# Two token groups, 128 and 160 wide, at the ends and openings of the stages of a decoder trunk

## The chip, the core and the metric

The kernel runs on one core of one Trainium2 chip. A core has a matrix engine (TensorE, "PE" in the rows, with its weight loads listed apart as "PEld"), a vector engine (VectorE, "DVE"), an activation engine (ScalarE, "ACT"), GpSimd ("POOL") and queues for transfers (SP, and the queues of ACT and POOL). The metric is the device time of one execution in microseconds (us); less is better.

## The reference

One step of a two-layer decoder trunk over 288 token columns: 256 tokens of a prompt and 32 tokens of a sample group (8 sequences of 4). Everything is float32.

```python
for l in range(DEPTH):                       # DEPTH = 2
    h = rms_norm(x, norm_mix_pre[l])
    m = pool_sgu_mixer(h, ...) if l % 2 == 0 else retention_mixer(h, ...)
    x = x + rms_norm(m, norm_mix_post[l])
    h = rms_norm(x, norm_ffn_pre[l])
    f = conv_ffn(h, ...)                     # gelu(conv(h @ w_gate)) * (h @ w_up) @ w_down
    x = x + rms_norm(f, norm_ffn_post[l])

def rms_norm(x, g):
    return x * lax.rsqrt(jnp.mean(x * x, axis=-1, keepdims=True) + EPS) * g
```

What matters here: between two stages stands a norm over all 2048 features of a token, so the first product of a stage needs the last product of the stage before, for the same token. Different tokens don't need each other in a norm.

## The kernel before

Features lie on the partitions (16 tiles of 128) and the 288 tokens on the free axis. `xbuf` (tiles `x[k]`) holds the residual, `mbuf` (`m`) the output of a stage before its norm, `hh[k]` and `hl[k]` the rounded part and the rest of the normed input of a stage. Every product is made in blocks of 128 x 128 weights. `mm3` (L198) makes three matmuls of a block: rounded weights by rounded input (L201), rounded weights by the rest of the input (L203, or L205 where it is put off to the end of a first pass), rest of the weights by rounded input (L206). All three move 288 columns, each with a weight load of its own of 128 columns. There are 6928 blocks; their weights come in chunks of 8 blocks (512 KB) in one fixed order, written out by `block` (L152): ACT rounds a chunk (`whi`, L134) and DVE takes the rest (`wlo`, L141), up to four chunks ahead (`wsp`, 4 buffers).

`product` (L212) makes the output tiles of one product. The first `first` tiles (`acc_h`) run side by side, input tile by input tile, so that the matmuls of input tile kk follow as soon as `prep(kk)` has made that tile; the other tiles (`acc_n`) run one after the other. Work of the other engines is written into this stream by hand: `tick()` after each block steps generators that yield for a number of blocks.

Three times a stage ends in a norm and another one opens on it: the mixer of layer 0 into its feed-forward part, that into the retention mixer of layer 1, that into the second feed-forward part. A fourth end is that of the kernel. At each of them the last product (`add_out`, L381) squares its tiles and adds the squares up on POOL (`sqm`); `post_stat` (L359) sums the squares over the partitions by narrow matmuls (`rms_stat`, `st_ps`, L289 and L292), DVE and POOL make the inverse root (`ms` L295, `rs` L297), and `rms_bcast` spreads it over the partitions by matmuls (`rb_ps`, L306). In the meantime TensorE runs matmuls on zeros (`keep_warm`, L274; at the end of the retention mixer `final_state` of the last head, L820 to L822, stands in the place of two of the three groups). Then `entry` (L330) makes the input of the next stage tile by tile: DVE scales `m` by the norm (`pn`, L377), DVE or POOL adds it to `x` (L378), ACT makes `hh` (L342) and squares (L314), DVE makes `hl` (L345). The first five tiles of the next product (`HEAD = 5`) follow this through 16 passes, one for each input tile. The second norm (before a stage) is not waited for: it is made beside the last passes (`rb_side`) and multiplied into the outputs. At the end of the kernel the same scaling and adding (L987, L991) leads to the stores of `y` (L992).

Of the kernel before, what the change touches and what calls it, by code (L numbers as in the profile page):

```python
# [14 lines left out]
D = 2048  # L15
# [15 lines left out]
HEAD = 5  # L31
TAIL = ((0, 1, 1), (1, 1, 0), (2, 2, 1), (4, 1, 0), (5, 2, 1), (7, 1, 0), (8, 1, 0), (9, 2, 1), (11, 1, 0), (12, 1, 1), (13, 2, 0), (15, 1, 0))
# [74 lines left out]
def trunk(ctx: ExitStack, tc: tile.TileContext, i, o, g4, order):  # L107
# [13 lines left out]
    state = {"loaded": 0, "hi": 0, "lo": 0, "next": 0}  # L121
# [22 lines left out]
    def prefetch(loads, his, los):  # L144
        while state["loaded"] < min(loads, NCHUNK):
            load_chunk()
        while state["hi"] < min(his, NCHUNK):
            hi_chunk()
        while state["lo"] < min(los, NCHUNK):
            lo_chunk()  # L150

    def block(mat, kt, nt):  # L152
# [7 lines left out]
        if b == 1:  # L160
            prefetch(c + 7, c + 4, 0)
        if b == 5:
            prefetch(0, 0, c + 4)
        hi, lo = chunks[c]
        return hi[:, b * 128:(b + 1) * 128], lo[:, b * 128:(b + 1) * 128]
# [42 lines left out]

    def bank(name):
        return psum.tile([128, 512], F32, tag="ps", name=name)  # L210

    def product(nts, kts, rhs, evac, first=0, prep=None, begin=None):  # L212
# [3 lines left out]
        for kk, kt in enumerate(kts):  # L216
# [10 lines left out]
        for j in range(len(head), len(nts)):  # L227
# [7 lines left out]
        drain("evac")  # L235
# [49 lines left out]
    def rms_stat(parts):  # L285

        ps = bank("st_ps")
        zeros = wz.bitcast(F32)
        PE.matmul(ps[0:96, 0:6], zeros[:, 0:96], zeros[:, 0:6], start=True, stop=False)  # L289
        for n, sq in enumerate(parts):  # L290
            for t in range(3):
                PE.matmul(ps[0:96, 2 * t:2 * t + 2], sq[:, 96 * t:96 * t + 96], ones[:, 0:2],  # L292
                          start=False, stop=n == len(parts) - 1 and t == 2)
        ms = tmp.tile([96, 3], F32, tag="ms", name="ms")
        V.tensor_scalar(ms, ps[0:96, 0:6].rearrange("p (t c) -> p t c", c=2)[:, :, 0], 1.0 / D, EPS, op0=ALU.mult, op1=ALU.add)  # L295
        rs = tmp.tile([96, 3], F32, tag="rs", name="rs")
        G.tensor_tensor(rs, ms, mhalf[0:96, 0:3], op=ALU.pow)  # L297
        return rs

    def rms_bcast(rs):  # L300

        pb = bank("rb_ps")
        for t in range(3):
            r = rs[:, t:t + 1]
            r = bass.AP(tensor=r.tensor, offset=r.offset, ap=[list(r.ap[0]), [0, 128]])
            PE.matmul(pb[:, 96 * t:96 * t + 96], r, ident[0:96, 0:96], start=True, stop=True)  # L306
        return pb[:, 0:T]
# [22 lines left out]
    def entry(gain, update, ahead):  # L330

        sq = t288("sq2", tag="sq")
        box = []
        done = [0]

        def upto(n):
            while done[0] < min(n, KT + 2):
                k = done[0]
                if k < KT:
                    update(k)  # L340
                if 1 <= k <= KT:
                    A.activation(hh[k - 1], x[k - 1], AF.Copy, scale=col(gain, k - 1))  # L342
                    square_add(sq, x[k - 1], k - 1)
                if k >= 2:
                    V.scalar_tensor_tensor(hl[k - 2], x[k - 2], col(gain, k - 2), hh[k - 2].bitcast(F32),  # L345
                                           op0=ALU.mult, op1=ALU.subtract)
                done[0] += 1
                if done[0] == KT + 2:
                    side("fast", late(rb_side(sq, box)))
# [5 lines left out]
        def prep(kk):  # L355
            upto(kk + 3 + ahead)
        return prep, box

    def post_stat(parts, fill=None):  # L359
        drain("late")  # L360
        if fill:
            fill[0]()
        else:
            keep_warm(6)
        rs = rms_stat(parts)
        if fill:
            fill[1]()
        else:
            keep_warm(5)
        pb = rms_bcast(rs)  # L370
        keep_warm(7)
        return pb

    def post_update(pb):
        def update(k):
# [3 lines left out]
        return update  # L379

    def add_out(first, parts=None, gain=None):  # L381

        def evac(j, ps):
# [11 lines left out]
        def squared(j, ps):  # L395
            if j < KT - 1:
                yield 1
# [3 lines left out]
            elif j < KT - 1:  # L401
                square_add(parts[0], ps, j)
            else:
                s = t288("sqt", tag="t2")
                A.activation(s, ps, AF.Square)
                parts.append(s)
# [11 lines left out]
    with ExitStack() as l0:  # L418
        p0 = l0.enter_context(tc.tile_pool(name="p0", bufs=1))
        hid = l0.enter_context(tc.tile_pool(name="hid0", bufs=16))  # L420
        prep, rbox = entry("pre_mix0", lambda k: prefetch(3, (k + 1) // 3, k // 3), 2)
# [45 lines left out]
        def v_norm():  # L467
# [18 lines left out]
            for t, n in ((0, 128), (1, 128), (2, 32)):  # L486
                vt = vtok[0:n, t, :]
                V.tensor_tensor(vt, vt, sgb[0:n, :], op=ALU.add)
                yield 14
            G.dma_start(out=o["cv"], in_=vtok[0:32, 2, :])  # L490
# [43 lines left out]
        def mix(j):  # L534
            yield 3
            h = j // 2
            pm = bank("mix_ps")
# [26 lines left out]
        def begin_mix(j):  # L564
            if j >= 16:
# [3 lines left out]
                first=HEAD, prep=prep, begin=begin_mix)  # L569
# [10 lines left out]
        for gi in range(4):  # L580
# [3 lines left out]
        parts = []  # L584
# [6 lines left out]
    def ffn(l, pb):  # L591
        with ExitStack() as s:
            pf = s.enter_context(tc.tile_pool(name=f"pf{l}", bufs=1))
            hid = s.enter_context(tc.tile_pool(name=f"hidf{l}", bufs=GRP + 3))
            prep, rbox = entry(f"pre_ffn{l}", post_update(pb), 2)
# [5 lines left out]
            G.dma_start(out=cs, in_=i["conv"][l])  # L601
            for ex in exts:
                G.memset(ex[:, 0:2], 0.0)
            hsp, gl = {}, {}

# [37 lines left out]
            def pairs(fs, first=0, prep=None):  # L643
                product([(f"{w}{l}", f) for f in fs for w in ("gate", "up")], ALLK, hs,
                        lambda j, ps: (evac_gate, evac_up)[j % 2](fs[j // 2], ps), first=first, prep=prep)

            NG = FT // GRP
            parts = []
            for g in range(NG):
# [5 lines left out]
                if g + 1 < NG:  # L655
                    pairs([fs[-1] + 1])
                drain("late")
                product([(f"down{l}", n) for n in ALLK], fs, hsp, add_out(g == 0, parts if g == NG - 1 else None, f"post_ffn{l}"),
                        first=4 if g == NG - 1 else 0)
            G.dma_start(out=o["conv"][l], in_=co)  # L660
            return post_stat(parts)

    pb = ffn(0, pb)


    with ExitStack() as l1:
        hid = l1.enter_context(tc.tile_pool(name="hid1", bufs=8))
        p1 = l1.enter_context(tc.tile_pool(name="p1", bufs=1))
        prep, rbox = entry("pre_mix1", post_update(pb), 2)
# [5 lines left out]
        for e in range(2):  # L675
            qp = p1.tile([128, 2, 256], F32, tag=f"qpad{e}", name=f"qpad{e}")
            G.memset(qp, 0.0)
            qpads.append(qp)
# [4 lines left out]
        for w in (kst, kd, *vsts, *s2w):  # L683
            G.memset(w.bitcast(F32), 0.0)
# [12 lines left out]
        rot, tail = [], []  # L697
# [114 lines left out]
        def prompt_out(h, R):  # L812
# [28 lines left out]
            last = []  # L841

            def put_state(dt, pf):
                if h < HEADS - 1:
                    sf = p1.tile([128, 512], F32, tag="sf", name="sf")
                else:
                    if not last:
                        last.append(p1.tile([128, 4, 512], F32, tag="s0", name="sfl"))
                    sf = last[0][:, dt, :]
# [3 lines left out]
            if h == HEADS - 1:  # L853
                tail.append((final_state, put_state))
                return
# [222 lines left out]
```

## Time and profile before

| | |
|---|---|
| median of 3 runs | 2992.92 us (2991.96 to 2995.87) |
| the profiled execution: its own time | 2992.97 us |
| its span from the first to the last instruction | 2991.3 us |
| granted clock over the span | 0.999 of full speed |
| busy share of the span: PE, PEld, DVE, ACT, POOL | 99%, 97%, 61%, 40%, 11% |

A profile lists every instruction with its engine, its line in the kernel, its start and its duration. The listed duration of a matmul (0.29 us for 288 columns) has a modelled end and overlaps the next one; what a matmul costs in a stream is the distance from its start to the start of the next one. Matmuls on zeros count as busy, so a busy share of 99% says nothing of useful work.

### The profile page before, as it was taken

What the parts mean: (1) busy time and instruction counts of PE and PEld (TensorE: products, weight loads), DVE (VectorE), ACT (ScalarE), POOL (GpSimd) and SP (SyncE); (2) the same over time, 40 slices, a digit from 0 to 9 for tenths busy, and PEclk for the clock granted to TensorE, in tenths of its full rate; (3) what the DMA queues carried; (4) which work ended last, traced back from release to release, by engine and by line L of the source; (5) the groups of instructions that cost most, each with busy time, mean ns of one, the idle gap of its engine ahead of it and who ended that gap; (6) DMA issues with size and microseconds to landing.
All of it is one profiled execution on the core that took longest, in us unless ns stands there. A gap on an engine that the chain in (4) does not pass through costs nothing.

```text
span 2991.3 us, 53198 instructions
## 1 busy us (share of the span) xinstructions
PE 2955.7 (99%) x21960; PEld 2889.5 (97%) x21960; DVE 1818.1 (61%) x2698; ACT 1207.7 (40%) x1841; POOL 316.6 (11%) x571
## 2 busy tenths in 40 slices
PE   9999999999999999999999999999999999999998
PEld 9999999999999999998999999999999999999998
DVE  6754864664665657666556665666775565565654
ACT  5344434343333345443343343333633433333333
POOL 3502300000000014000000000000500000000003
PEclk9999999999999999999999999999999999999999
DMA  6444455555555554576757747656455555455553
GB/s 232 164 159 150 152 166 168 163 163 161 169 162 162 169 170 146 193 234 220 254 166 243 249 165 242 226 201 240 151 164 171 162 162 172 160 162 174 161 167 127
DMA packets 159284, 540.27 MB, mean 181 GB/s; under 512 B 15969, under 2 KB 21617, under 8 KB 159041
## 3 DMA queue, kind: packets, MB, share of 16 engines
q1 hardware_dynamic: 146720, 493.45, 50.3%
q0 software_dynamic: 11184, 42.38, 4.3%
q8 instruction: 172, 2.82, 0.4%
q10 hardware_dynamic: 1136, 1.04, 0.1%
q14 instruction: 72, 0.58, 0.1%
HBM read 495.20 MB, written 41.60 MB: 179 GB/s over the span
## 4 chain that ended last, share of the span: by engine, by line
PE 88%; DVE 6%; DMA 3%; issue 1%; ACT 1%; POOL 1%; SPq 0%; DVEq 0%; ACTq 0%; POOLq 0%
PE acc_n L201 27%; PE acc_n L206 26%; PE acc_n L203 26%; DVE wlo L141 2%; DMA s<-in_ret_dram 2%; PE acc_h L201 1%; PE acc_h L206 1%; PE acc_h L203 1%; DMA out_rets_dram<-s 1%; PE qi_ps L882 1%; DVE hl L345 1%; DVE s L891 1%; DVE pn L377 1%; PE sn_ps L888 0%; POOL dbl L508 0%
## 5 line engine op out<-in xcount | busy, mean ns | idle before, releaser
L141 DVE TENSOR_TENSOR wlo<-raw,whi 128x1024 fp32r<-128x1024 f32 x866 | 1067.8, 1241 | 643.6 <-ACT whi L134 635.7
L201 PE MATMUL acc_n<-hh,whi 128*128 128x288 f32 x4416 | 1315.9, 298 | 0.0
L203 PE MATMUL acc_n<-hl,whi 128*128 128x288 f32 x4416 | 1302.8, 295 | 0.0
L206 PE MATMUL acc_n<-hh,wlo 128*128 128x288 f32 x4416 | 1299.3, 294 | 1.6 <-DVE wlo L141 1.6
L134 ACT CAST whi<-raw 128x1024 fp32r<-128x1024 f32 x866 | 896.3, 1046 | 842.6 <-PE acc_n L203 609.7
L201 PEld LDWEIGHTS acc_n<-hh,whi 128*128 128x128 f32 x4416 | 827.9, 187 | 6.9 <-issue 5.1
L206 PEld LDWEIGHTS acc_n<-hh,wlo 128*128 128x128 f32 x4416 | 831.5, 188 | 2.0 <-DVE wlo L141 2.0
L203 PEld LDWEIGHTS acc_n<-hl,whi 128*128 128x128 f32 x4416 | 829.4, 188 | 1.3
L201 PE MATMUL acc_n<-fhi,whi 128*128 128x288 f32 x1320 | 389.6, 295 | 0.0
L203 PE MATMUL acc_n<-flo,whi 128*128 128x288 f32 x1320 | 389.5, 295 | 0.0
L206 PE MATMUL acc_n<-fhi,wlo 128*128 128x288 f32 x1320 | 388.8, 295 | 0.0
L206 PEld LDWEIGHTS acc_n<-fhi,wlo 128*128 128x128 f32 x1320 | 248.4, 188 | 0.0
L203 PEld LDWEIGHTS acc_n<-flo,whi 128*128 128x128 f32 x1320 | 247.8, 188 | 0.0
L201 PEld LDWEIGHTS acc_n<-fhi,whi 128*128 128x128 f32 x1320 | 247.4, 187 | 0.0
L624 ACT ACTIVATE gg<-cv 128x256 f32<-128x256 f32 x88 | 36.8, 418 | 382.1 <-DVE cv L622 382.1
L614 POOL COPY co<-fext 128x16 f32<-128x16 f32 x88 | 17.4, 198 | 1430.8 <-DVE fext L612 1430.8
L201 PE MATMUL acc_n<-rhi,whi 128*128 128x288 f32 x496 | 147.4, 297 | 0.0
L203 PE MATMUL acc_n<-rlo,whi 128*128 128x288 f32 x496 | 146.3, 295 | 0.0
L206 PE MATMUL acc_n<-rhi,wlo 128*128 128x288 f32 x496 | 146.2, 295 | 0.0
L891 DVE SCALAR_TENSOR_TENSOR s<-s,sn_ps 128x512 f32<-128x512 f32 x128 | 81.1, 681 | 76.8 <-PE sn_ps L888 76.8
L388 DVE TENSOR_TENSOR mbuf<-mbuf,acc_n 128x288 f32<-128x288 f32 x128 | 57.5, 452 | 113.3 <-PE acc_n L206 113.3
L203 PE MATMUL acc_h<-hl,whi 128*128 128x288 f32 x300 | 90.5, 302 | 11.6 <-DVE hl L345 11.5
(271 smaller groups left out, 2895.0 us busy)
## 6 DMA issues: line engine op xcount, KB each, us to landing
raw<-in_w_dram SPq DMA_DIRECT2D x866, 512.0 KB, 3.6
s<-in_ret_dram SPq DMA_DIRECT2D x32, 1024.0 KB, 6.5
out_rets_dram<-s POOLq DMA_DIRECT2D x32, 1024.0 KB, 6.0
out_retp_dram<-sf POOLq DMA_DIRECT2D x14, 256.0 KB, 2.6
xbuf<-in_x_dram SPq DMA_DIRECT2D x3, 576.0 KB, 6.6
hc<-in_hc_dram SPq DMA_DIRECT2D x8, 177.0 KB, 5.3
out_y_dram<-xbuf SPq DMA_DIRECT2D x3, 288.0 KB, 2.2
out_conv_dram<-co POOLq DMA_DIRECT2D x2, 396.0 KB, 3.5
```

The lines of the kernel that those rows point to most:

```text
L134: A.copy(hi, raws[c])
L141: V.tensor_tensor(lo, raws.pop(c), hi.bitcast(F32), op=ALU.subtract)
L201: PE.matmul(ps, wh, xh, start=start, stop=False)
L203: PE.matmul(ps, wh, xl, start=False, stop=False)
L206: PE.matmul(ps, wl, xh, start=False, stop=stop)
L345: V.scalar_tensor_tensor(hl[k - 2], x[k - 2], col(gain, k - 2), hh[k - 2].bitcast(F32), op0=ALU.mult, op1=ALU.subtract)
L377: V.tensor_tensor(t, m[:, k, :], pb, op=ALU.mult)
L388: V.tensor_tensor(m[:, j, :], m[:, j, :], ps, op=ALU.add)
L614: G.tensor_copy(co[:, f, 0:NB, :], exs[:, :, DS:])
L624: A.activation(g[:, 0:SEQ], c[:, 0:SEQ], AF.Gelu_apprx_tanh)
L882: PE.matmul(pi[32 * g:32 * g + 32, :], qp[:, dt, 32 * b:32 * b + 32], s0[:, g, :], start=n == 0, stop=False, tile_position=(0, 32 * g))
L891: V.scalar_tensor_tensor(s0[:, g, :], s0[:, g, :], g4[h], pns[g], op0=ALU.mult, op1=ALU.add)
```

## The change

The tokens are split into two groups, columns 0 to 127 and 128 to 287 (`HALVES`). At the end of a stage the last tiles of the last product (two, of the retention mixer five) first run for all their blocks on group 0 and then again, with the same weights, on group 1; beside the matmuls of group 1 the norm of group 0 is made and its first four input tiles for the next stage. In the opening the first four passes (`K1 = 4`, now over six tiles, `HEAD = 6`) run for group 0, beside which the norm of group 1 is made, and then for group 1. The other twelve passes have all 288 columns in one matmul again. The matmuls on zeros at the three boundaries go, and so do those between the last matmul and the first sum at the end of the kernel. Weights that a second pass needs again are held (`state["hold"]`). In the entry of a stage the additions to `x` of the first four tiles are all DVE's; in the other twelve passes DVE scales a tile in two instructions, one for each group, since the two norms lie in two banks. The final states of the last retention head are made where those of the other heads are. At the end of the kernel, group 0 is scaled and added beside the statistics of group 1, and the tail of 12 steps becomes one of 6 stores. The first product of the kernel is as before (`HEAD - 1`), and `mix` waits in program order for the normed `v`.

```diff
-HEAD = 5
-TAIL = ((0, 1, 1), (1, 1, 0), (2, 2, 1), (4, 1, 0), (5, 2, 1), (7, 1, 0), (8, 1, 0), (9, 2, 1), (11, 1, 0), (12, 1, 1), (13, 2, 0), (15, 1, 0))
+HEAD = 6
+K1 = 4
+HALVES = ((0, 128, 128), (128, T, 80))
...
+    def mm3_half(ps, w, rhs, h, start, stop):
+        c0, c1, _ = HALVES[h]
+        (wh, wl), (xh, xl) = w, rhs
+        if start is None:
+            PE.matmul(ps, wh, xh, start=True, stop=False)
+            ps = ps[:, c0:c1]
+        else:
+            PE.matmul(ps, wh, xh[:, c0:c1], start=start, stop=False)
+        PE.matmul(ps, wh, xl[:, c0:c1], start=False, stop=False)
+        PE.matmul(ps, wl, xh[:, c0:c1], start=False, stop=stop)
+
+    def halves(work, chain, evac=None):
...
+        n0 = state["next"]
+        state["hold"] = min(n0 // CH + 4, NCHUNK)
+        ws = []
+        for h in range(2):
+            ch = chain(h)
+            for n, (psums, blk, rhs, start, stop, before) in enumerate(work):
+                if before is not None:
+                    before(h)
+                next(ch, None)
+                if h == 0:
+                    ws.append(block(*blk))
+                else:
+                    c, b = divmod(n0 + n, CH)
+                    state["hold"] = min(c + 4, NCHUNK)
+                    ahead(c, b)
+                mm3_half(psums[h], ws[n], rhs, h, start[h], stop)
+                tick()
+                if evac is not None and stop:
+                    evac(n, psums[h], h)
+            for _ in ch:
+                pass
+        state["hold"] = NCHUNK
...
-        for kk, kt in enumerate(kts):
+        if opening is not None:
+            work = []
+            for kk in range(K1):
...
+            halves(work, opening)
+        for kk, kt in list(enumerate(kts))[K1 if opening is not None else 0:]:
...
-    def rms_stat(parts):
+    def rms_stat(parts, c0=0, c1=T, g=96):
...
-    def post_stat(parts, fill=None):
-        drain("late")
-        if fill:
-            fill[0]()
-        else:
-            keep_warm(6)
-        rs = rms_stat(parts)
-        if fill:
-            fill[1]()
-        else:
-            keep_warm(5)
-        pb = rms_bcast(rs)
-        keep_warm(7)
-        return pb
...
+    class Boundary:
...
         def update(self, k, h):
             t = t288("pn")
-            V.tensor_tensor(t, m[:, k, :], pb, op=ALU.mult)
-            (V if k < 2 or k % 2 else G).tensor_tensor(x[k], x[k], t, op=ALU.add)
+            for e in range(2):
+                if h in (e, None):
+                    c0, c1, _ = HALVES[e]
+                    V.tensor_tensor(t[:, c0:c1], m[:, k, c0:c1], self.pb[e], op=ALU.mult)
+            c0, c1 = HALVES[h][:2] if h is not None else (0, T)
+            (V if h is not None or k % 2 else G).tensor_tensor(x[k][:, c0:c1], x[k][:, c0:c1], t[:, c0:c1], op=ALU.add)
...
+        def ending(self):
+            for _ in range(6):
+                yield
+            rs = rms_stat(self.sums(), *HALVES[0])
+            V.memset(hh[0][:, HALVES[1][0]:].bitcast(F32), 0.0)
+            for _ in range(7):
+                yield
+            self.pb.append(rms_bcast(rs, *HALVES[0]))
+            for _ in range(self.lead):
+                self.advance()
+                yield
+                yield
...
+        def opening(self, h):
+            if h == 0:
+                for _ in range(5):
+                    yield
+                rs = rms_stat(self.sums(), *HALVES[1])
+                for _ in range(7):
+                    yield
+                self.pb.append(rms_bcast(rs, *HALVES[1]))
...
-                add_out(True, parts, "post_mix0"), first=4)
-        pb = post_stat(parts)
+                add_out(True, bd, "post_mix0"), first=4, ending=(2, bd.ending))
...
+                        first=4 if end else 0, ending=(2, end.ending) if end else None)
...
+                    first=4 if end else 0, ending=(5, end.ending) if end else None)
...
+    last.scale(0, 8, 4)
+    last.scale(0, 12, 4)
+    for k, eng in ((0, G), (4, G), (8, V), (12, V)):
+        last.add(eng, 0, k, 4)
+    last.pb.append(rms_bcast(rs, *HALVES[1]))
+    for n, (k, w, eng) in enumerate(((0, 4, G), (4, 2, G), (6, 4, V), (10, 2, G), (12, 2, V), (14, 2, V))):
+        last.scale(1, k, w)
+        last.add(eng, 1, k, w)
+        (nc.sync if n % 2 else A).dma_start(out=yr[:, k:k + w, :], in_=xbuf[:, k:k + w, :])
```

## Rows read from the trace of the kernel before

**Rows 1.** The page of the profile: the first line of its part on engines (busy us, share of the span, instructions) and the first line of its chain of waits (share of the span by engine).
```profile
PE 2955.7 (99%) x21960; PEld 2889.5 (97%) x21960; DVE 1818.1 (61%) x2698; ACT 1207.7 (40%) x1841; POOL 316.6 (11%) x571
...
PE 88%; DVE 6%; DMA 3%; issue 1%; ACT 1%; POOL 1%; SPq 0%; DVEq 0%; ACTq 0%; POOLq 0%
```

**Rows 2.** TensorE in order of time (start, duration, engine, line, operation), around the first boundary: the last matmul of the mixer of layer 0, the first zeros, the first matmul of the next product, the first matmul after its head.
```profile
287.72 0.30 PE L206 MATMUL acc_n<-ahi,wlo 128*128 128x288 f32 x1
287.85 0.64 PE L274 MATMUL warm<-wz 128*128 128x512 f32 x2
...
294.24 0.40 PE L201 MATMUL acc_h<-hh,whi 128*128 128x288 f32 x1
...
332.97 0.29 PE L201 MATMUL acc_n<-hh,whi 128*128 128x288 f32 x1
```

**Rows 3.** TensorE in order of time, the same places of the second and the third boundary; at the third the last product is followed at once by the matmuls of the last head's final states (the first and the sixth of twelve are shown).
```profile
1145.11 0.29 PE L206 MATMUL acc_n<-fhi,wlo 128*128 128x288 f32 x1
...
1190.35 0.29 PE L201 MATMUL acc_n<-hh,whi 128*128 128x288 f32 x1
...
2115.25 0.40 PE L820 MATMUL sf_ps<-vth,kzh 128*128 128x512 f32 x1
...
2116.41 0.39 PE L822 MATMUL sf_ps<-vth,kzl 128*128 128x512 f32 x1
...
2160.83 0.29 PE L201 MATMUL acc_n<-hh,whi 128*128 128x288 f32 x1
```

**Rows 4.** TensorE in order of time in a plain stream of 288 columns: two matmuls with 24 starts between them (at the end of the last product; the second is the kernel's last full matmul).
```profile
2969.77 0.29 PE L206 MATMUL acc_n<-fhi,wlo 128*128 128x288 f32 x1
...
2972.97 0.29 PE L206 MATMUL acc_n<-fhi,wlo 128*128 128x288 f32 x1
```

**Rows 5.** Weight loads in order of time. First four loads of 128 columns for matmuls that move only 32 columns, and the two loads that follow; then the two loads with which a head resumes after the stall of the first boundary.
```profile
1209.78 0.53 PEld L766 LDWEIGHTS sc_ps<-qk,kd 128*128 128x128 f32 x4
1210.23 0.19 PEld L201 LDWEIGHTS acc_n<-hh,whi 128*128 128x128 f32 x1
1210.34 0.19 PEld L203 LDWEIGHTS acc_n<-hl,whi 128*128 128x128 f32 x1
...
294.23 0.19 PEld L201 LDWEIGHTS acc_h<-hh,whi 128*128 128x128 f32 x1 [0.39 <-ACT hh L342]
294.34 0.19 PEld L206 LDWEIGHTS acc_h<-hh,wlo 128*128 128x128 f32 x1
```

**Rows 6.** TensorE in order of time: four matmuls that move 256 columns of plain float32, and the four of 128 columns that follow at once.
```profile
1208.58 1.02 PE L762 MATMUL sc_ps<-qk 128*128 128x256 f32 x4
1209.44 0.61 PE L764 MATMUL sc_ps<-qk 128*128 128x128 f32 x4
```

**Rows 7.** TensorE in order of time: six narrow matmuls (weights of 96 columns, two columns moved) and the spreading matmuls of the second norm, beside the head of the first boundary; between them the group of the narrow ones over the span (count, busy us, mean ns of one, idle before).
```profile
328.53 0.65 PE L292 MATMUL st_ps<-ones,sq 128*96 128x2 f32 x6
...
L292 PE MATMUL st_ps<-ones,sq 128*96 128x2 f32 x24 | 2.6, 224 | 0.0
...
331.10 0.80 PE L306 MATMUL rb_ps<-cst,rs 96*128 96x96 f32 x6
```

**Rows 8.** Two stretches of the head of the first boundary: length, busy us and number of instructions of PE, PEld, DVE, ACT and POOL, granted clock, busy share of the DMA engines, GB/s.
```profile
300.00:310.00 10.00, 9.02 (x68) 8.79 (x67) 9.93 (x14) 5.99 (x12) 7.56 (x7) 1.00 0.32 106
310.00:320.00 10.00, 9.51 (x70) 9.04 (x69) 9.93 (x14) 6.27 (x12) 6.42 (x7) 1.00 0.46 158
```

**Rows 9.** DVE's groups of instructions from 300 to 328 us, within that head (line, operation, count, busy us, mean ns of one, idle before), and the one wait of TensorE between 294 and 333 us (us in total, times, longest).
```profile
L141 DVE TENSOR_TENSOR wlo<-raw,whi 128x1024 fp32r<-128x1024 f32 x8 | 14.0, 1750 | 0.0
L345 DVE SCALAR_TENSOR_TENSOR hl<-xbuf,vec,hh 128x288 fp32r<-128x288 f32 x13 | 9.8, 760 | 0.0
L377 DVE TENSOR_TENSOR pn<-mbuf,rb_ps 128x288 f32<-128x288 f32 x10 | 4.4, 441 | 0.0
L378 DVE TENSOR_TENSOR xbuf<-xbuf,pn 128x288 f32<-128x288 f32 x5 | 2.9, 587 | 0.2
...
PE acc_h L203 <- DVE hl L345: 3.9, 6, 1.5
```

**Rows 10.** The end of the kernel in order of time: the sum's first step on DVE, the inverse root on POOL, the first and the last instructions of the scaling and adding.
```profile
2975.80 0.16 DVE L295 TENSOR_SCALAR ms<-st_ps 96x3 f32<-96x3 f32 x1 [2.04 <-PE st_ps L292]
2976.05 0.88 POOL L297 TENSOR_TENSOR rs<-ms,mhalf 96x3 f32<-96x3 f32 x1 [4.66 <-DVE ms L295]
2977.93 1.48 DVE L987 TENSOR_TENSOR mbuf<-mbuf,rb_ps 128x288 f32<-128x288 f32 x3 [1.98 <-PE rb_ps L306]
...
2979.31 8.34 SPq L992 DMA_DIRECT2D out_y_dram<-xbuf  x6
...
2986.50 1.11 DVE L991 TENSOR_TENSOR xbuf<-xbuf,mbuf 128x576 f32<-128x576 f32 x2
```

**Rows 11.** The groups of scaling and adding at the end (as in rows 9), and the DMA view from 2977 us: packets and bytes.
```profile
L991 POOL TENSOR_TENSOR xbuf<-xbuf,mbuf 128x576 f32<-128x576 f32 x3 | 4.7, 1571 | 1.3 <-DVE mbuf L987 1.3
L987 DVE TENSOR_TENSOR mbuf<-mbuf,rb_ps 128x288 f32<-128x288 f32 x8 | 3.3, 444 | 2.0 <-PE rb_ps L306 2.0
L987 DVE TENSOR_TENSOR mbuf<-mbuf,rb_ps 128x576 f32<-128x576 f32 x4 | 3.0, 743 | 0.0
...
DMA packets 2240, 2.36 MB, mean 157 GB/s; under 512 B 192, under 2 KB 2240, under 8 KB 2240
```

**Rows 12.** One stretch of that end, columns as in rows 8.
```profile
2982.00:2983.00 1.00, 0.00 (x0) 0.00 (x0) 1.00 (x3) 0.00 (x0) 0.62 (x1) 1.00 0.99 347
```

More of the change, by code (lines that the diff above doesn't have):

```diff
@@ L226, in product @@
             side("evac", evacuate(evac, j, ps[j], gap))
-        for j in range(len(head), len(nts)):
+        last = len(nts) - (ending[0] if ending else 0)
+        for j in range(len(head), last):
             m_, n = nts[j]
@@ L234, in product, with __init__, __getitem__, chain @@
             side("evac", evacuate(evac, j, p, gap))
-        drain("evac")
+        if ending is None:
+            drain("evac")
+            return
+        work = []
+        banks = {}
+        class Half:
+            def __init__(self, j):
+                self.j = j
+            def __getitem__(self, h):
+                if (self.j, h) not in banks:
+                    banks[self.j, h] = bank("acc_s")[:, 0:HALVES[h][1] - HALVES[h][0]]
+                return banks[self.j, h]
+        for j in range(last, len(nts)):
+            m_, n = nts[j]
+            for kk, kt in enumerate(kts):
+                work.append((Half(j), (m_, kt, n), rhs[kt], (kk == 0,) * 2, kk == len(kts) - 1, None))
+        def chain(h):
+            if h == 1:
+                drain("evac", "late")
+                yield from ending[1]()
+        halves(work, chain, lambda n, p, h: evac(last + n // len(kts), p, h))
     def evacuate(evac, j, p, gap):
@@ L657, in ffn @@
                 drain("late")
[L658 to L663, printed above, removed]
+                end = Boundary(after) if g == NG - 1 else None
+                if end:
+                    G.dma_start(out=o["conv"][l], in_=co)
+                product([(f"down{l}", n) for n in ALLK], fs, hsp, add_out(g == 0, end, f"post_ffn{l}"),
+                        first=4 if end else 0, ending=(2, end.ending) if end else None)
+            return end
+    bd = ffn(0, bd, "pre_mix1")
     with ExitStack() as l1:
@@ L696, in trunk @@
         osp = {}
-        rot, tail = [], []
+        rot = []
         def rope(dst, a, b):
@@ L939, in evac @@
                     do_v(h, R, j - 4, ps)
-            product(nts, ALLK, hs, evac, first=HEAD if h == 0 else 0, prep=prep if h == 0 else None)
+            product(nts, ALLK, hs, evac, first=HEAD if h == 0 else 0, prep=prep if h == 0 else None,
+                    opening=bd.opening if h == 0 else None)
             return R
@@ L957, in out_part @@
                 assert step("slow") or ks[-1] in osp
-            product([("ret_out", n) for n in ALLK], ks, osp, add_out(heads[0] == 0, parts, "post_mix1"),
-                    first=4 if parts is not None else 0)
-        parts = []
+            product([("ret_out", n) for n in ALLK], ks, osp, add_out(heads[0] == 0, end, "post_mix1"),
+                    first=4 if end else 0, ending=(5, end.ending) if end else None)
         for h in range(HEADS):
```

240 lines of the change are left out of this document (142 added, 98 removed).

## The prediction, made before the change was run

> **What bounds the kernel now.** I read the shares of the engines first: TensorE is busy 99% of the span and holds 88% of the chain of waits [rows 1]. That says only that it is always issuing something, zeros among it. So I read TensorE in order of time at the four places that the change touches. At the first boundary the last useful matmul starts at 287.72 us and would be followed by another at 287.85; the next useful one starts at 294.24 and the first one behind the head at 332.97 [rows 2]. In a plain stream a matmul of 288 columns takes (2972.97 − 2969.77) / 24 = 0.1333 us [rows 4]. The head holds 5 tiles x 16 passes x 3 = 240 matmuls, 32.0 us at that pace, and the matmuls of the second norm, some 8 at 0.085 and 6 at 0.11, 1.3 us [rows 7]. Of the 45.12 us from 287.85 to 332.97, 11.8 are therefore lost: 6.4 before the head and 5.4 within it. The second boundary (1145.24 to 1190.35) loses 11.8 as well; the third (2115.25 to 2160.83) does useful work in the stall, twelve matmuls of final states at (2116.41 − 2115.25) / 5 = 0.232, 2.8 us, and loses 9.5 [rows 3]. The end of the kernel takes from 2973.10 to the end of the span at 2991.3, 18.2 us [rows 4]. So 33.1 us at the boundaries and a part of 18.2 is all that can be won.
>
> Within a head the reader is to see that DVE is the bound: 9.93 us busy in each 10, while TensorE issues 138 matmuls (68 and 70) in 20 us where 150 would fit, and waits for `hl` [rows 8, 9]. A pass takes 2.0 + 5.4/15 = 2.36 us, of DVE's work.
>
> Elsewhere the change touches nothing that binds: the first product and the plain streams stay, making the last head's final states costs the same 2.8 us in its new place, and the order in which `mix` follows the normed `v` is that of the instructions before, within a few blocks.
>
> **The change part by part. (a) Split matmuls.** Blocks that run twice: at the ends 2 x 16 = 32, 2 x 11 = 22, 5 x 4 = 20 and 2 x 11 = 22, in the openings 4 passes x 6 tiles = 24 at each of three. That is 168 blocks, 504 matmuls of 288 columns that become 1008 of 128 or 160, each with a weight load of its own of 128 columns. All of it lies on TensorE, the engine that sets the time. What does a narrow one cost? If only columns counted, 0.0629 and 0.077 (from 0.1333 at 288 and 0.232 at 512 columns, 0.00044 a column [rows 3, 4]), together hardly more than one whole one. But four matmuls that move 32 columns are spaced by their loads: (1210.23 − 1209.78) / 4 = 0.1125 us for a load of 128 columns [rows 5]; with weights of 96 columns it is (0.65 − 0.224)/5 = 0.085 [rows 7]. Those weights are plain float32; the rounded ones of this product load no faster: the first two loads after a stall start 0.11 apart (294.23, 294.34), where the second had nothing else to wait for [rows 5]. I take 0.112 for either group. In the plain stream this load is hidden behind 0.1333 of columns; behind 0.063 or 0.077 it is not. A split costs 2 x 0.112 − 0.1333 = 0.0907 us, 504 of them 45.7 us: 15.2 at the first boundary (56 blocks), 12.5 at the second (46), 12.0 at the third (44), 6.0 at the end (22). Bounds: 0.105, the least that the starts 0.11 apart can be, read to hundredths, gives 38.7; 0.1333 each, no gain from being narrow, gives 67.2.
>
> A rule of the Trainium skill speaks for the change here: the page "TensorE: Matmul & The Clock Gate", section "Back-to-back issue gap", has pairs of load and matmul of 128 columns sustained at about 81 ns; by it, taken for both groups, a split would cost 0.029 and all of them 14.4 us, an estimate. The same page, section "LDWEIGHTS (loading the stationary operand)", has a load at columns divided by 1.2 ns, 107 ns for 128, with which the trace's 0.1125 and 0.11 agree [rows 5].
>
> **(b) The norms themselves** leave the stall but not TensorE: at an ending three sums in two float32 passes with loads of 128 columns, 6 x 0.112, and two spreading ones, 0.22; in the opening 14 with loads of 80 columns, 14 x 0.071 (0.085 x 80/96), and 4 x 0.11. That is 0.9 + 1.45 = 2.35 at each boundary, 0.9 more at the kernel's end.
>
> **(c) The stall before the head** goes, 6.4 us twice and some 4 at the third, if each norm is ready when TensorE comes to it. The chain from the sums to the spread is `ms` 0.16, the root 0.88 and hops, some 1.2 us (2975.80 to 2976.93 at the end [rows 10]); it has 7 blocks of 0.336, 2.35 us, and before it 5 or 6 blocks, 1.7 to 2.0 us, for the last tile to be added and squared, at worst behind one of ACT's roundings of weights. That fits mostly; I put 0.8 us a boundary for where it doesn't (0 to 3).
>
> **(d) The head's own loss.** Four passes are now two half passes each, 18 x 0.112 = 2.0 us of TensorE; DVE's part of one, scaling (0.27 to 0.31), adding and `hl`, is about 1.1 and 0.66 of weights (only three chunks in these eight, since weights are held), so TensorE is the bound there. In the other twelve passes TensorE has 18 x 0.1333 = 2.4 us; DVE has its 2.36, an eighth of a chunk more (0.22 at 1.75 [rows 9]) and a second scaling instruction (0.13), 2.71. Its lag of 0.31 x 12 = 3.7 us less one tile of lead: I take 2.5 us (0, if the lead is larger, to 5.5, as now).
>
> **(e) The end.** Before, 2.8 us pass from the last matmul to `ms`, and scaling begins at 2977.93; DVE ends at 2987.61, and 3.7 us later the span ends [rows 10]. After, the zeros ahead of the sums are gone and the last piece is narrower, `ms` at about 1.65 us, the second norm at 3.6; but DVE then still has four of group 0's instructions (512 elements, 0.68 each from 0.444 at 288 and 0.743 at 576 [rows 11]), so group 1 begins at 4.6, has nine instructions of 0.31 to 0.82, 5.2 us, and ends near 10 instead of 14.6: 4.5 us won. Against it, no store can begin before POOL has added the first four tiles twice (1.4 and 1.75, after two others), at about 7.4, later than now (2979.31, 6.3), and 2.36 MB then go at the 347 GB/s at which the DMA engines are full here [rows 12], 6.8 us, so that the end comes 1.7 us sooner than now. I take 2.5, nearer to the stores.
>
> **The sum.** First boundary 15.2 + 2.35 + 0.8 + 2.5 = 20.9 instead of 11.8, +9.1; second 18.2 instead of 11.8, +6.4; third 17.7 instead of 9.5, +8.2; end 6.0 + 0.9 − 2.5 = +4.4. Together +28 us on the 2992.97 of the profiled execution, which is within 0.05 of the median of the runs: 3021.
>
> **The rivals.** *The load is not the bound of a narrow matmul* (the other side). If loads overlapped enough that columns alone counted, a split would cost 0.14 − 0.1333 = 0.0066 and all 3.3 us: 3021 − 42 = 2979, faster. It decides where a pair takes less than 0.168 us (0.1333 + 17.6/504, with 17.6 what all but the splits gains), 0.084 a piece. For it speaks only that no row here has a narrow matmul with rounded weights; against it are the 0.11 between loads after a stall and 0.1125 in the narrow group [rows 5]. By the page's 81 ns it would be about 2990, an estimate. *Narrow is not shorter at all.* Plain float32 of 256 columns takes (1209.44 − 1208.58)/4 = 0.215 [rows 6], 0.00084 a column, twice the 0.00044 of the rounded ones; if rounded ones fell back to that when narrow, 0.112 and 0.134 give +11, 3032; at 0.1333 each it is 3042. *The wait moves instead of going.* If TensorE still waits at each norm (3 us) and DVE's lag is as large as now (5.5), the three boundaries give 5.2 us more each, 3037. *The change doesn't do what it says*: if group 0's first tiles were not ready at the opening, a part of the 6.4 us would stand beside the loads; that is the same 3037.
>
> **How the numbers follow.** The load is the bound with 88%: forecast 3021, its own range from 38.7 for the splits, no lag, no waits and 4.5 at the end (3021 − 7 − 10 − 2 = 3002) to the moved waits (3037). Columns alone 5%, something between, near the page's 81 ns, 3%, narrow not shorter 4%. Range 3002 to 3038. A difference of under 0.2%, 6 us, is about what a measurement of this kernel cannot tell from none. Faster by more: 0.06 (the first rival); within: 0.04; slower: 0.90.
>
> **What would show it.** In the profile of the changed kernel: the starts of the split matmuls 0.11 apart, weight loads back to back (0.063 to 0.08 would prove the first rival, 0.133 the second); no zeros and hardly a wait between the last tile and the head, in which case (c) holds; DVE still at 9.9 of 10 us and TensorE waiting for `hl` in the twelve whole passes, but under 5.4 us; the end from the last matmul to the span's end 2 to 4 us shorter. The prediction is wrong if the 1008 pieces take under 80 us, or if the losses in heads and stalls don't fall by at least half.

## The result, and the profile after

The changed kernel takes 3029.72 us (median of 4 runs, 3024.47 to 3047.17) where the kernel before takes 2993.76 (4 runs): 1.0129 times as long, 95% interval 1.0113 to 1.0145. The forecast was 3021, within 3002 to 3038. The profiled execution took 3024.47 us, its span went from 2991.3 to 3022.7, by 31.4. The median lies 5 us above that execution because two of the four runs were longer, 3034.78 and 3047.17; their mean granted clocks were 0.992 and 0.988, those of the other two 0.997 and 0.996.

The page of the changed kernel, its lines on engines and on the chain of waits by engine, beside [rows 1]:

```profile
PE 2989.1 (99%) x22432; PEld 2929.2 (97%) x22432; DVE 1826.7 (60%) x2786; ACT 1215.2 (40%) x1875; POOL 312.8 (10%) x571
...
PE 93%; DVE 3%; DMA 2%; issue 1%; POOL 1%; ACT 0%; SPq 0%; DVEq 0%; ACTq 0%; POOLq 0%
```

TensorE is as busy as before, but holds 93% of the chain, not 88%, and DVE 3%, not 6%: waits have become matmuls. How long these are is in TensorE's own order of time, here at the first boundary and, from 2997 us on, at the end:

```profile
274.89 0.22 PE L220 MATMUL acc_s<-ahi,whi 128*128 128x128 f32 x1
...
275.73 0.27 PE L222 MATMUL acc_s<-ahi,wlo 128*128 128x128 f32 x1
...
276.96 0.28 PE L221 MATMUL acc_s<-blo,whi 128*128 128x128 f32 x1
...
297.19 0.33 PE L217 MATMUL acc_h<-hh,whi 128*128 128x288 f32 x1
...
346.50 0.38 PE L205 MATMUL acc_n<-hh,whi 128*128 128x288 f32 x1
...
2997.74 0.28 PE L221 MATMUL acc_s<-flo,whi 128*128 128x160 f32 x1
...
2998.52 0.28 PE L222 MATMUL acc_s<-fhi,wlo 128*128 128x160 f32 x1
```

Between 275.73 and 276.96 lie 11 starts, 0.112 us each, for 128 columns; between 2997.74 and 2998.52 seven, 0.111 each, for 160. A quarter more columns cost nothing. The weight loads of the same stretch, six starts between these two, keep the same distance:

```profile
275.89 0.19 PEld L221 LDWEIGHTS acc_s<-alo,whi 128*128 128x128 f32 x1
...
276.56 0.19 PEld L221 LDWEIGHTS acc_s<-alo,whi 128*128 128x128 f32 x1
```

Where the time went, stretch by stretch, on equal work (whole blocks at 3 x 0.1333 us taken out of each, and the second norm):

| stretch | lost before | lost after | forecast after |
|---|---|---|---|
| first boundary (after: 274.89 to 346.50) | 11.8 | 19.1 | 20.9 |
| second boundary (1143.66 to 1207.56) | 11.8 | 15.4 | 18.2 |
| third boundary (2128.28 to 2192.14) | 9.5 | 16.2 | 17.7 |
| end (2989.29 to 3022.7, less 22 blocks) | 18.2 | 24.6 | 22.6 |
| retention mixer between its head and its last tiles (after: 1207.56 to 2128.28) | 0 | 7.4 | 0 |

The stalls of 6.4 us are gone: from 274.89 to 313.5 us TensorE is busy without a gap. The DVE lag of the heads [rows 8, 9] is nearly gone too. The last row of the table was forecast at nothing. It too is on equal work: 36 blocks fewer lie in that stretch than before, and the last head's final states, 2.8 us, lie there now. TensorE's longest waits show where it comes from (us in total, times, longest):

```profile
PE ot_ps L1051 <- DVE on L1069: 5.0, 2, 4.7
...
PE acc_h L207 <- DVE hl L442: 1.7, 4, 0.5
```

The same place in order of time, all engines: two transposes, the DVE instruction that the third wants, and the ten that waited for it. In the kernel before these stand at 1311.85 and 1312.91 us, with an idle time of 0.68.

```profile
1323.46 0.44 PE L1051 MATMUL ot_ps<-cst,on 128*128 128x128 f32 x2
...
1327.73 0.81 DVE L1069 TENSOR_SCALAR on<-qi_ps,mv,lr 128x512 f32<-128x512 f32 x1 [0.68 <-POOL lr L564]
...
1328.60 2.40 PE L1051 MATMUL ot_ps<-cst,on 128*128 128x128 f32 x10 [4.70 <-DVE on L1069]
```

And three stretches (columns as in rows 8, the granted clock third from the right): the whole passes of the first head, and the time behind and before 1327.1 us.

```profile
313.50:342.80 29.30, 28.45 (x215) 27.98 (x215) 27.72 (x43) 18.07 (x31) 17.51 (x20) 1.00 0.50 171
1327.10:1334.00 6.90, 5.40 (x22) 5.12 (x23) 4.20 (x11) 1.29 (x3) 0.56 (x1) 0.51 0.65 199
1320.00:1327.10 7.10, 3.64 (x26) 1.84 (x24) 4.77 (x9) 0.27 (x1) 0.75 (x1) 1.00 0.50 186
```

In the whole passes TensorE issues 215 matmuls in 29.30 us, 0.136 each, beside a DVE that is busy 27.72. In the mixer it is busy 3.64 of 7.10 us up to 1327.1, then still in its wait (1323.90 to 1328.60), and there its clock falls to its lower level (1.2 GHz) for 6.9 us: of these, 5.4 lie behind the wait, and what runs in them takes about twice as long. So the wait cost more than its own 4.7 us.

The end of the kernel, instructions in order of time:

```profile
3004.89 0.24 PE L367 MATMUL st_ps<-wz 128*80 128x4 f32 x2
...
3007.23 2.48 POOL L507 TENSOR_TENSOR xbuf<-xbuf,mbuf 128x512 f32<-128x512 f32 x2
...
3007.59 3.27 DVE L507 TENSOR_TENSOR xbuf<-xbuf,mbuf 128x512 f32<-128x512 f32 x2
3010.78 1.94 DVE L502 TENSOR_TENSOR mbuf<-mbuf,rb_ps 128x640 f32<-128x640 f32 x3
...
3013.24 2.95 ACTq L1140 DMA_DIRECT2D out_y_dram<-xbuf  x3
...
3016.21 0.49 DVE L507 TENSOR_TENSOR xbuf<-xbuf,mbuf 128x320 f32<-128x320 f32 x1
```

And what the transfers moved from 3005 us to the end, in 40 slices of 0.44 us, from the view of the DMA engines:

```profile
GB/s 0 0 0 0 0 0 0 0 0 0 0 0 0 0 0 0 0 0 0 0 200 356 310 343 353 353 333 348 369 328 366 351 356 346 356 177 0 0 0 0
```

DVE's two additions for group 0 take 1.6 us each beside POOL's two, not the 0.68 forecast (which was read from scalings, L987 [rows 11]); group 1 begins 5.9 us behind the last matmul, not 4.6; the first store is issued at 8.35, not 7.4; and from then on the transfers run without a gap, at 310 to 369 GB/s. From the last matmul to the end it is 17.8 us instead of 18.2.

### The profile page after: what moved, and what is told of

The parts are those of the page before. It is cut to its first block, busy times and chain, and to the rows that moved or that the text cites. A ratio compares the mean times of both kernels' runs of the same rounds, so it can differ in the third digit from the quotient of the medians.

```text
span 3022.7 us, 54246 instructions
## 1 busy us (share of the span) xinstructions
PE 2989.1 (99%) x22432; PEld 2929.2 (97%) x22432; DVE 1826.7 (60%) x2786; ACT 1215.2 (40%) x1875; POOL 312.8 (10%) x571
## 4 chain that ended last, share of the span: by engine, by line
PE 93%; DVE 3%; DMA 2%; issue 1%; POOL 1%; ACT 0%; SPq 0%; DVEq 0%; ACTq 0%; POOLq 0%
PE acc_n L205 27%; PE acc_n L210 26%; PE acc_n L207 26%; PE acc_h L210 2%; PE acc_h L205 2%; PE acc_h L207 2%; DVE wlo L142 1%; PE qi_ps L1031 1%; DMA s<-in_ret_dram 1%; PE acc_s L222 1%; PE acc_s L221 1%; PE acc_s L220 1%; PE acc_h L222 1%; DVE s L1040 1%; PE acc_h L221 1%
## 5 line engine op out<-in xcount | busy, mean ns | idle before, releaser
L205 PE MATMUL acc_n<-hh,whi 128*128 128x288 f32 x4368 | 1302.3, 298 | 0.0
L207 PE MATMUL acc_n<-hl,whi 128*128 128x288 f32 x4368 | 1289.0, 295 | 0.0
L210 PE MATMUL acc_n<-hh,wlo 128*128 128x288 f32 x4368 | 1285.5, 294 | 1.6 <-DVE wlo L142 1.6
L205 PEld LDWEIGHTS acc_n<-hh,whi 128*128 128x128 f32 x4368 | 819.2, 188 | 6.7 <-issue 4.6
L210 PEld LDWEIGHTS acc_n<-hh,wlo 128*128 128x128 f32 x4368 | 822.9, 188 | 2.1 <-DVE wlo L142 2.1
L207 PEld LDWEIGHTS acc_n<-hl,whi 128*128 128x128 f32 x4368 | 820.7, 188 | 1.4
L205 PE MATMUL acc_n<-fhi,whi 128*128 128x288 f32 x1276 | 376.5, 295 | 0.0
L207 PE MATMUL acc_n<-flo,whi 128*128 128x288 f32 x1276 | 376.5, 295 | 0.0
L210 PE MATMUL acc_n<-fhi,wlo 128*128 128x288 f32 x1276 | 375.9, 295 | 0.0
L205 PEld LDWEIGHTS acc_n<-rhi,whi 128*128 128x128 f32 x476 | 89.5, 188 | 2.6 <-issue 2.2
```

What stands on the lines that cost most here:

```text
L205: PE.matmul(ps, wh, xh, start=start, stop=False)
L207: PE.matmul(ps, wh, xl, start=False, stop=False)
L210: PE.matmul(ps, wl, xh, start=False, stop=stop)
```

## The experiments

The theory after this: the split costs what its weight loads cost; the 7.4 us of the mixer come from the longer head alone; and what the median lies above the profiled run goes with the clock. Rivals stand with each run. The first four shared a chip and 15 runs of the kernel before (median 2995.56), the last four another one and 7 runs (2993.59). Between chips the ratio to the kernel before is the better measure.

**The wait in the mixer.** `e1_pace` is the changed kernel with one number changed, `e2_head6` the kernel before with the longer heads alone, `e3_head6_pace` both of these edits.

```diff
-            pace = 16 if h < HEADS - 1 else 12
+            pace = 16 if 0 < h < HEADS - 1 else 12
```

```diff
-HEAD = 5
+HEAD = 6
...
-                first=HEAD, prep=prep, begin=begin_mix)
+                first=HEAD - 1, prep=prep, begin=begin_mix)
```

> The changed kernel with one number changed: the state units of the first retention head wait 12 blocks after each unit, not 16. Theory: the longer head (6 tiles, not 5) leaves 16 blocks fewer between the start of these units and the point in the second head's gates where they are written out in one piece; 4 units x 4 blocks give the 16 back, so the 4.7 us wait of TensorE for the normed output (on, L1069) goes and the retention mixer gets about 7 us shorter: 3017 us, and with the wait the fall of the granted clock behind it goes, so that the runs lie within 0.2% of one another instead of 0.75%. Rival: the mixer got longer for another reason (the last head's final states, their banks), and the wait only moves: 3023 to 3027, with the spread as it was.

Measured: 3018.48 us (3015.58 to 3019.01), 1.0074 times the kernel before (1.0059 to 1.0089). The span fell from 3022.7 to 3015.8, the mixer's loss from 7.4 to 0.4 (1207.75 to 2121.47), the runs lie within 0.11% of one another at clocks of 0.997 and 0.998, and the wait is down to this:

```profile
PE ot_ps L1051 <- DVE on L1069: 1.4, 2, 1.1
```

> The kernel before with one part of the change alone: six tiles instead of five in the three heads behind a norm; no split. Theory: a pass of a head goes from 2.0 to 2.4 us of TensorE beside 2.36 + 0.22 = 2.58 us of DVE, so the lag behind DVE falls from 5.4 to about 2.9 us a boundary, 7.5 us less in all, and the wait for on in the retention mixer appears here too, 7 us more: 2993 us, about as before. Rival (the split is what lengthens the mixer): no such wait, 2985 us.

Measured: 2990.82 us, 0.9984 times (0.9974 to 0.9993). The wait for `on` is there, 4.7 us at the longest, and within it the clock falls, for 6.8 us, without any split. The three boundaries are 3.4, 3.4 and 3.3 us shorter on equal work: the lag behind DVE fell from 5.4 to 2.0, more than expected. The mixer is 8.4 us longer.

> As the run before, and the first retention head's units 16 blocks earlier in all. Theory: the gain of the longer heads without the wait: 2985.5 us, faster than the kernel before by 0.25%. Rival: the longer head is not what makes the wait, then as the run before.

Measured: 2985.76 us, 0.9970 times (0.9957 to 0.9982). This one beats both kernels, the one before by 0.3%: 9.8 us by the medians, 6.6 by the spans of the profiled executions (2984.7 against 2991.3). The boundaries there are 10 us shorter, but the mixer is still 4.1 us longer than before, not 8.4: TensorE waits for the states' transfers (`s<-in_ret_dram`) 6.4 us in all, against 2.7 before and 4.7 in `e2_head6`. What makes these waits longer was not tested. The head of its first boundary, from the first matmul on zeros to the first behind the head, takes 48.09 us with 16 blocks (6.4 us) more in it, 41.7 on equal work against 45.12 [rows 2]:

```profile
287.43 0.40 PE L274 MATMUL warm<-wz 128*128 128x512 f32 x1
...
335.52 0.29 PE L201 MATMUL acc_n<-hh,whi 128*128 128x288 f32 x1
```

A stretch of its passes (columns as in rows 8) has 149 matmuls in 20 us where the kernel before has 138, while DVE is still full: six tiles to a pass give TensorE about as much work as DVE has.

```profile
300.00:320.00 20.00, 19.72 (x149) 19.48 (x148) 19.90 (x26) 12.27 (x23) 14.38 (x13) 1.00 0.47 157
```

So the longer head is what made the wait for `on`: the head of the mixer's first product holds one tile (16 blocks) more, and as many fewer blocks lie between the start of the first head's state units and the second head's gates, where what is left of these units is written out at once, without the blocks between that used to cover DVE's chain. And `e1_pace` against `e3_head6_pace`, 3018.48 against 2985.76 on one chip, is the price of the split with all that the change brings besides it (the new end, DVE's two scalings and its additions, the moved final states): 33 us.

**The load as the bound.** The runs above don't tell a load's 0.112 from columns that happen to cost as much. Groups of 64 and 224 columns do:

```diff
-HALVES = ((0, 128, 128), (128, T, 80))
+HALVES = ((0, 64, 64), (64, T, 112))
```

> The changed kernel with the 12 blocks of the first run here, and groups of 64 and 224 columns instead of 128 and 160. Theory (the weight load of 128 columns sets the distance): matmuls of 64 columns are spaced 0.111 us like those of 128, those of 224 0.112 to 0.115, and the time stays within 3 us of the first run of these. Rival (columns set it, with something fixed): 64 columns come at well under 0.1 us, 224 at 0.12 or more.

Measured: 3061.2 us (one run), 43 more than the first of these runs. TensorE in order of time, pairs of 64 columns, of 64 columns later in the same run, and of 224 columns:

```profile
276.77 0.28 PE L220 MATMUL acc_s<-ahi,whi 128*128 128x64 f32 x1
...
278.00 0.28 PE L222 MATMUL acc_s<-bhi,wlo 128*128 128x64 f32 x1
...
284.68 0.40 PE L220 MATMUL acc_s<-bhi,whi 128*128 128x64 f32 x1
...
286.18 0.40 PE L221 MATMUL acc_s<-blo,whi 128*128 128x64 f32 x1
...
300.79 0.28 PE L220 MATMUL acc_s<-ahi,whi 128*128 128x224 f32 x1
...
301.91 0.27 PE L221 MATMUL acc_s<-alo,whi 128*128 128x224 f32 x1
```

64 columns start 0.112 apart (11 starts in 1.23 us), 224 columns 0.112 too (10 in 1.12): the load is the bound from 64 to 224 columns, as the theory has it. That it is not a fixed price of every pair is seen in loads of fewer columns. In the changed kernel, weight loads in order of time, twelve loads of 80 columns of plain float32 for matmuls that move two, and the load that follows:

```profile
299.04 0.37 PEld L370 LDWEIGHTS st_ps<-ones,sqm 128*80 128x80 f32 x4
299.32 0.65 PEld L370 LDWEIGHTS st_ps<-ones,sqs 128*80 128x80 f32 x8
299.90 0.19 PEld L217 LDWEIGHTS acc_h<-hh,whi 128*128 128x128 f32 x1
```

They start 0.072 apart (12 in 0.86 us), those of 96 columns 0.085 [rows 7], those of 128 columns 0.112: the distance goes with the columns loaded. Rounded weights are loaded in 128 columns only here. The time was missed, and the second pair of `e4_widths` shows why: 0.214 apart (7 in 1.50). Two stretches of that run (columns as in rows 8, the granted clock third from the right):

```profile
275.50:281.40 5.90, 5.90 (x56) 5.90 (x54) 1.23 (x1) 2.15 (x5) 1.46 (x1) 1.00 0.54 180
281.40:294.20 12.80, 12.80 (x63) 12.80 (x62) 0.00 (x0) 0.45 (x3) 0.00 (x0) 0.50 0.00 0
```

After 5.9 us of matmuls of 64 columns, with TensorE never idle, the clock went to 1.2 GHz, and load and matmul with it. The same happened at each boundary and at the end. Up to the last matmul the clock is down for 95 us in all, in which about half as many matmuls start as at the higher level, which covers the 43 us.

**The clock.** The changed kernel itself, once more, on the second chip:

> The changed kernel once more, beside the others of this call, to see whether its spread of 0.75% comes back. Theory: the wait of 4.7 us in the retention mixer and the fall of the granted clock behind it are the whole of it, and the clock falls here for longer in some runs: median 3024 to 3031, a mean granted clock of 0.988 to 0.997, above the first run with the pace of 12 by 6 to 12 us. Rival: the spread was that of one chip: 3024 to 3026 in all runs.

Measured: 3028.68 us, 1.0113 times (1.0092 to 1.0133): 3023.11, 3033.39, 3023.97 and 3034.03, at clocks of 0.997, 0.992, 0.997 and 0.992. The spread came back and goes with the clock. Whether the chip has a part in it stays open: the chip of the first four runs of the changed kernel is not on record, `e1_pace` had no spread on the first chip of these, and the next run has one on the second. The expectation that the wait in the mixer is the whole of it didn't hold, as the next run shows, in which the wait for `on` is at most 1.1 us.

```diff
-                        first=4 if end else 0, ending=(2, end.ending) if end else None)
+                        first=4 if end else 0, ending=(2, end.ending) if end and after else None)
...
+    drain("late")
+    keep_warm(6)
+    rs = rms_stat(last.parts)
+    keep_warm(5)
+    pb = rms_bcast(rs)
+    keep_warm(7)
+    for n in range(len(TAIL) + 1):
...
```

> The run with the pace of 12, with the kernel's end as before the change: last two tiles unsplit, zeros, 288 columns scaled and added in the old tail. The splits there cost 66 x 0.09 = 6.0 us and the first norm 0.9; the profile of the changed kernel has the stretch behind the last matmul only 0.4 us shorter (17.8 instead of 18.2), for its stores go out in one piece at 350 GB/s from 13.9 to 20.3 us behind it. Theory: 3018.5 - 6.4 = 3012 us. Rival: the early part of the work on group 0 does shorten the end, and its loss is paid again: 3015 to 3018.

Measured: 3009.63 us in one run, at a clock of 0.998, and 3021.63 to 3024.28 in three, at 0.993 and 0.994; median 3022.62. The profiled one is of the longer ones. Its end, from the last matmul on, takes 18.2 us as in the kernel before, 6.4 less than the split end on equal work, as the theory has it, and 3009.63, a single run on the other chip, is 6.0 below the lowest run of `e1_pace`. (The expectation places the stores of the changed kernel from 13.9 to 20.3 us behind its last matmul; in the DMA view above they lie from about 9 to 16 us behind it.) Its other time is at the third boundary, where both kernels have the same instructions. First two stretches of this run, then the same two of `e1_pace`, 0.9 us earlier there (columns as in rows 8):

```profile
2122.40:2142.10 19.70, 19.69 (x181) 19.50 (x179) 11.07 (x29) 14.12 (x34) 8.18 (x12) 1.00 0.33 106
2142.10:2169.40 27.30, 27.30 (x128) 27.30 (x127) 15.08 (x34) 9.04 (x19) 8.45 (x13) 0.50 0.22 73
```

```profile
2121.50:2141.20 19.70, 19.70 (x180) 19.52 (x179) 11.07 (x29) 14.11 (x34) 8.17 (x12) 1.00 0.32 106
2141.20:2168.50 27.30, 26.97 (x221) 26.73 (x220) 25.38 (x51) 16.53 (x31) 15.20 (x19) 1.00 0.39 131
```

The first stretches are alike to a matmul or two, narrow ones all the way and no wait of TensorE. In the one run the clock then falls for 27.3 us and TensorE issues 128 matmuls, in the other it stays and 221 are issued; the boundary ends 11.6 us later. Why it falls in one of them was not found. The median of `e5_plain_end` was missed by this.

**How many passes to split.** `e6_two_passes` splits two passes of each opening, `e7_endings_only` none.

```diff
-K1 = 4
+K1 = 2
```

> The run with the pace of 12, with two split passes in each opening instead of four (K1 = 2). 12 blocks fewer are split at each of three boundaries, 36 x 3 x 0.09 = 9.8 us less; the second norm then has only 12 blocks before it is wanted, and its first tile comes about 2 us late at each, 6 us. Theory: 3014 to 3015 us. Rival (a split costs nearly nothing, the waits make the loss): 3022 or more.

Measured: 3030.34 us (3025.54 to 3030.87), 1.0115 times (1.0100 to 1.0130): 12 more than `e1_pace`, not 4 less, at clocks of 0.992 and 0.993. The expected wait is there, of 1.3 and then 0.3 us, and as the longer one ends the clock falls; the first boundary, TensorE's longest wait in the window 296 to 316 us and two stretches:

```profile
PE acc_h L220 <- ACT hh L433: 1.3, 1, 1.3
```

```profile
297.10:304.10 7.00, 5.80 (x56) 5.65 (x55) 2.81 (x8) 2.20 (x6) 1.63 (x1) 1.00 0.51 176
304.10:314.30 10.20, 9.81 (x43) 9.60 (x44) 7.74 (x19) 4.47 (x11) 7.33 (x11) 0.50 0.25 67
```

It fell at all three boundaries, for 10.2, 13.7 and 10.2 us, each time in a narrow stream with a wait of about 1 us shortly before. The wait for the second norm is not always what came first: at the second boundary the clock fell at 1167.6 us, 5 us behind a wait for `hl` and before the wait for `hh` (TensorE in order of time, with the idle time in front):

```profile
1162.59 0.33 PE L221 MATMUL acc_h<-hl,whi 128*128 128x128 f32 x1 [1.12 <-DVE hl L442]
...
1170.03 0.50 PE L220 MATMUL acc_h<-hh,whi 128*128 128x160 f32 x1 [1.29 <-ACT hh L433]
```

Since the clock also falls without a wait (`e4_widths`, `e5_plain_end`), that the waits make it fall is not shown. The rival of that run named 3022 or more, but for waits alone; the rows show short waits and a low clock, with narrow matmuls still some 0.112 apart where it is up. What two passes would cost at full clock this run doesn't tell.

```diff
         if opening is not None:
+            keep_warm(4)
+            for n, _ in enumerate(opening(0)):
+                if n == 5:
+                    keep_warm(5)
+            keep_warm(7)
+            opening = None
+        if opening is not None:
```

> The run with the pace of 12, with the openings unsplit: the ends run in two groups as before, then TensorE waits, with zeros, for the norm of group 1, and all 16 passes of the heads have 288 columns. Removes 72 of the split blocks, 19.6 us; brings back a stall of about 5 us at each boundary, 15 us, in which the sums and spreads (1.45 us each, 4.4 in all) lie that stood on TensorE. Theory: 3018.5 - 19.6 + 15 - 4.4 = 3009 us, and 3 us more if DVE lags in the first passes, so 3009 to 3012. Rival (the openings pay for themselves): 3019 or more.

Measured: 3015.31 us (3012.93 to 3016.25), 1.0069 times (1.0053 to 1.0086), more than the 3009 to 3012 expected and less than the rival's 3019; its span is 3011.2 against 3015.8. The first stall takes 5.26 us, as expected (from the first zeros at 297.14 to the head at 302.40), but the boundaries are only 1.1, 0.5 and 0 us shorter than with four split passes. The heads lose another 3.2, 2.3 and 1.9 us, TensorE waiting for DVE's `hl`, where the expectation had 3 us for all three; and at the third boundary the clock fell for 3.4 us and the stall takes 8.0. Most of the rest of the shorter span lies in the mixer, 2.7 us, where the waits for the states' transfers are 0.5 us instead of 2.8. Between chips the ratios 1.0069 and 1.0074 can't be told apart. Splitting the openings neither pays nor costs anything that these runs could show; most of the loss stays with the endings and the end when the openings are whole.

## Why the prediction was right, and where its steps were not

**(a) Split matmuls** was right in kind and size: 0.112 us forecast, 0.111 to 0.112 measured for 128 and 160 columns, some 45 us in all, the largest term of the sum. The first rival, that columns alone count, fell with the equal distances of 128 and 160 columns, and again with those of 64 and 224 in `e4_widths`. The 81 ns of the Trainium skill (page "TensorE: Matmul & The Clock Gate", section "Back-to-back issue gap") are not borne out for this product of rounded float32, at 111 to 112 ns; its rule for loads (the same page, section "LDWEIGHTS (loading the stationary operand)"), columns divided by 1.2 ns, is, at 107 against 112 measured.

**(b)** held: the narrow sums and spreads stand in TensorE's stream at the cost forecast, the 192 narrow matmuls and the first norm of the first ending taking 22.3 us (274.89 to 297.19) of a forecast 192 x 0.112 + 0.9 = 22.4.

**(c) and (d)** were right in direction and too dear. Waits and lag were put at 3.3 us a boundary; the first head takes 49.3 us (297.19 to 346.50) where its matmuls and norms make 47.7, so 1.6, the others about 0.6 and 1.9. The mis-sized term is DVE's time for a pass: 2.71 us was forecast against TensorE's 2.4. In the whole passes of the first head DVE is busy 27.72 us beside 215 matmuls, 2.3 us for each pass of 18, and they come at 0.136 us a matmul, 2.45: DVE is hardly the bound there any more. Neither of the two signs of being wrong came: the 1008 pieces take some 112 us, not under 80, and stalls and lag fell from 33 to about 4 us.

**(e) The end** was put at 2.5 us won and won 0.4. The bound named there, the stores, is what decided; what was mis-sized is when they can begin, since DVE's additions take 1.6 us, not 0.68, while POOL adds too. The sign named for this part, an end 2 to 4 us shorter, did not come.

**The step that failed** is the sentence that elsewhere the change touches nothing that binds. Six tiles in a head instead of five cost the retention mixer 7.4 us, a wait for `on` and the clock that fell in it; `e2_head6` shows it without a split, `e1_pace` takes it away. Blocks are the unit in which this kernel times its side work, and a tile moved into a head is 16 blocks taken from whatever counts them afterwards.

**What no step had** is the clock in the narrow stretches themselves. It can explain the runs above the profiled one: in `e5_plain_end` the same instructions as in `e1_pace` run 11.6 us longer at one boundary when it falls. That the changed kernel's own longer runs lost their 10 and 23 us in just these places is likely but not shown; only shorter ones were profiled.

The forecast of 3021 was thus 28 us for boundaries and end, which took 24, with a mixer at 0, which took 7.4, and with the clock, some 5 us of the median, left out. That it came within 4 us of the profiled execution is in part luck: waits and lag came out 6 us less than forecast and the end 2 us more, and the 7.4 us of the mixer more than made up for the difference.

## What to carry to other kernels

Before a matmul is split along the moved columns, put its weight load beside it: here a load of 128 columns takes 0.112 us, a matmul of 288 hides it and none of 64 to 224 does, so that each split of a whole matmul cost 0.09 us, and all that stalls and lag had cost at the three boundaries (33 us) was worth less than the 45 us of loads. The cheaper way to a wait on another engine was here to give TensorE more work of full width beside it: one tile more in the heads, with the pace put right, took 10 us off the boundaries and 7 to 10 off the kernel. When work moves past side work that is timed by counting blocks, count those blocks again.

## What the runs showed of the hardware that had not been expected

TensorE's granted clock fell from 2.4 to 1.2 GHz while the engine was never idle, in streams of matmuls whose loads were the bound: after 5.9 us of 64 columns, and once after 19.7 us of 128 and 160. In `e6_two_passes` it fell in such streams at all three boundaries, at most some 5 us behind a wait of 1.1 to 1.3. While it is down a narrow matmul takes 0.214 us instead of 0.112, its load included, and in these streams it stayed down for 6.8 to 27.3 us. The same instructions kept the clock in `e1_pace` and lost it in `e5_plain_end`, and no run here shows what decides. In the kernel before, with waits of up to 1.5 us in streams of 288 columns, it stayed up until the stores at the end.
